# A two-layer diffusion backbone: the last two expert groups combined in one accumulation, and the next layer's sum of squares taken behind the branch

## The chip, the cores and the metric
The kernel runs on 1 core of a Trainium2 chip. The metric is the device time of one execution in microseconds (us); lower is better. Before the change the median of 3 runs is 1619.9 us (1619.38 to 1620.89).

## The reference
Two layers act on 256 latent tokens and 256 context tokens of width 1024. Each layer norms and modulates its input, projects it, runs three token mixers, adds the result to the stream, norms again and runs a mixture of 32 experts. Cut to what the change touches:

```python
for l in range(DEPTH):                       # 2
    h = modulate(rms_norm(x, g_norm[l, 0]), sh1, sc1)
    y = token_mixers(h, hc, w_in[l], ...)    # h @ w_in first
    x = x + gt1 * y
    h = modulate(rms_norm(x, g_norm[l, 1]), sh2, sc2)
    x = x + gt2 * hier_moe(h, ...)           # top-1 group, top-2 experts
```

`rms_norm` needs the sum of x*x over the 1024 features of every token; `hier_moe` is the sum over experts of weight times SwiGLU expert. The context tokens go through the same steps in layer 0, with their own modulation.

## The kernel before
The stream x is held transposed in SBUF, as eight slices (k or f = 0 to 7) of 128 features by 512 tokens, in buffers named qkv. `mixers(l, ...)` does the norm, the projections and the mixers; `moe(l, ...)` does the experts. The order of instructions on each engine is set by a scheduler that simulates the program as it is recorded; the order of the code is only its starting point. SP issues the weight loads, in its own order.

**The experts.** Tokens are gathered into fixed slots, four experts to a group q, eight groups. `gate_up`, `swiglu`, `act_T` and `down(q)` (L1375) give each expert's rows `ys[q, v_]`, split in two parts; `combine(q)` (L1266) multiplies them by the scatter matrix `Cs[q]` into PSUM (L1275, TensorE, PE), and VectorE (DVE) adds the scaled result to x (L1280): 16 adds for a group of layer 0. The loop over q (L1403) runs `down(q - 1)` and `combine(q - 1)` inside group q; `down` and `combine` of the last group follow it (L1428, L1429).

**The end of layer 0.** Behind the last combine stand the preparation of layer 1's first weight chunk, win[1, 12] (L1431: split in whi by ScalarE, ACT, L230, and wlo by DVE, L231), and two `mod_chunk` (L1432 to L1435). A `mod_chunk` makes a piece of the modulation vectors: 8 matmuls of the conditioning with a weight tile (L247), a copy by ACT (L250), a pair of transposes (L252) and two small DVE operations (L256, L257). More chunks are put between later projections. In the trace one of these fp32 matmul instructions leaves two records.

**The overflow branch.** If a slot overflows, all experts are computed densely (the `If` of L1440). All engines test the same value and jump over the body when nothing overflows, as here. An engine passes the branch when its own work ahead of it is issued.

**The sum of squares.** `Stats.step` (L276) squares one slice on ACT (L279, L282) and adds it to `acc` (L286) on DVE or, for every second slice, on GpSimd (POOL). For layer 1 `combine` of the last group of layer 0 calls it after each slice of x is final (L1282), so it lies ahead of the branch, and the body of the branch does it again:

```python
                if nxt[0] is not None:
                    nxt[0].step(xT[f])
```

`Stats.cols` sums over the features by matmuls with ones (L295), then DVE (L299) and POOL (L302, the power -1/2); `Stats.rows` spreads the result over the partitions (L310) and ACT copies it to SBUF (L314). This is r, the row of 1/rms.

**The start of layer 1** (L474 to L485). x is written to DRAM as xs by two DMAs on ACT's queue (L1510). `scaled` makes h0 and l0, the two parts of x times the norm's gain and modulation, without r (L379 on ACT, L380 on DVE), so that the projection with win[1, 12] (48 matmuls L343, L344, L345 on qkv with whi and wlo; `mm3` does hi*hi, hi*lo, lo*hi) can run before r is known; its result is multiplied by r when it is read out (L730, then L754). `shift_share` (L409, L413, L415, L417) gives what the shift adds to it. `shifted` makes the normed h proper, in two parts hh and hl: x times r (L332, on DVE and POOL in turn), scale and shift (L337 on ACT, L339 on DVE), the split (L388 on ACT, L389 on DVE). All later projections of the layer read h; the first of them is with chunk win[1, 13]. SP loads three modulation weights into buffers y (L737) and three into wraw (L213) meanwhile.

Of the kernel before, what the change touches and what calls it, by code (L numbers as in the profile page):

```python
# [11 lines left out]
F32R = mybir.dt.float32r  # L12
# [7 lines left out]
DEPTH = 2  # L20
D = 1024
LAT = 256
CTX = 256
N = LAT + CTX
KT = D // 128
# [20 lines left out]
def tile_backbone(ctx: ExitStack, tc: tile.TileContext, T, out):  # L46
# [316 lines left out]
    def prep(src):  # L363
        return wsplit(wraw(src, [KT, 256]), [KT, 256])

    def mixers(l, need_ctx, xsrc, stats):
        nq = N if need_ctx else LAT
        ntq = nq // 128

# [52 lines left out]
        if l == 0:  # L422
            def mod_w(m, tag):
                w = s8(tag, [KT, 256]) if tag else wraw(T["wmod"][0, m], [KT, 256])
                if tag:
                    nc.sync.dma_start(w, T["wmod"][0, m])
                return w

            def split(w, hi, lo):
                for i in range(0, KT, 2):  # L430
                    h, o = (t.tiles[i // t.per][:, i % t.per:i % t.per + 2] for t in (hi, lo))
                    nc.scalar.copy(h, w[:, i:i + 2])
                    nc.vector.tensor_sub(o, w[:, i:i + 2], h.bitcast(F32))
                return hi, lo

            X[0] = x = slabs("mg", N)

            def load_x2(i):
                nc.sync.dma_start(x.tiles[i // 2][:, 2 * (i % 2):2 * (i % 2) + 2], T["xT"][:, 2 * i:2 * i + 2])

            wm = {4: mod_w(4, "h")}
            w0 = wraw(win[12], [KT, 256])
            load_x2(0)
            wm[5] = mod_w(5, "h")
            load_x2(1)
            w1 = wraw(win[13], [KT, 256])
            load_x2(2)
            wm[6] = mod_w(6, "h")
            load_x2(3)
            wm[7] = mod_w(7, "h")  # L450
            h0 = Slabs([s8("qkv", [4, N], F32R) for _ in range(2)], 4)
            l0 = Slabs([s8("qkv", [4, N], F32R) for _ in range(2)], 4)
            stats = Stats(N, False)
            mod_chunk(0, 4, pat, wm[4])
            pre_w = [split(w0, Slabs([s8("qkv", [KT, 256], F32R)], KT), Slabs([
                tp.tile([128, 4, 256], F32R, tag="PT", name=nm("wl"), bufs=PTB) for _ in range(2)], 4))]
            for j in range(4):
                if j > 0:
                    mod_chunk(0, 4 + j, pat, wm[4 + j])
                scaled((2 * j, 2 * j + 1))  # L460
                if j == 1:
                    pre_w.append(split(w1, Slabs([s8("y", [KT, 256], F32R)], KT),
                                       Slabs([s8("y", [KT, 256], F32R)], KT)))
                for k in (2 * j, 2 * j + 1):
                    stats.step(x[k], False)
            r = stats.rows(stats.cols(pao()), "acc", 1)
            hh, hl = full_norm()
            for j in range(4):
                mod_chunk(0, j, pat, mod_w(j, None))
                shift_parts(slice(2 * j, 2 * j + 2))  # L470
                shifted((2 * j, 2 * j + 1))
            for c in range(len(pre_w)):
                shift_share(c, pre_w[c])
        else:  # L474
            x = X[0]
            h0 = Slabs([s8("qkv", [4, N], F32R) for _ in range(2)], 4)
            l0 = Slabs([s8("qkv", [4, N], F32R) for _ in range(2)], 4)
            shift_parts(slice(0, KT))
            w, A = lead.pop()
            pre_w = [w]  # L480
            scaled(range(KT), A)
            r = stats.rows(stats.cols(pao()), "acc", 1)
            shift_share(0, pre_w[0])
            hh, hl = full_norm()
            shifted(range(KT), A)  # L485
# [265 lines left out]
        for f in shares:  # L751
            for v_ in range(2):
                c = slice(256 * v_, 256 * v_ + 256)
# [251 lines left out]
        xT = X[0]  # L1005
# [155 lines left out]
    def moe(l, nt, st, rt):  # L1161
# [99 lines left out]
                    nc.vector.scalar_tensor_tensor(  # L1261
                        htl[i][:, j, c], rt.tok[i][:, j, c], r, hth[i][:, j, c].bitcast(F32), op0=ALU.mult, op1=ALU.subtract)
        ys, Cs, ths = {}, {}, {}
        nxt = [None]

        def combine(q):  # L1266

            if l == 0 and q == NQ - 1:
                nxt[0] = Stats(nt, False)
            for f in range(KT):  # L1270
                p = pmm()
                for v_ in range(ns):
                    c = slice(256 * v_, 256 * v_ + 256)
                    for part in range(2):
                        nc.tensor.matmul(  # L1275
                            p[:, c], lhsT=ys[q, v_][:, part, 128 * f:128 * f + 128], rhs=Cs[q][:, c],
                            start=(part == 0), stop=(part == 1))
                for v_ in range(ns):
                    c = slice(256 * v_, 256 * v_ + 256)
                    nc.vector.scalar_tensor_tensor(  # L1280
                        xT[f][:, c], p[:, c], modT[l][:, 40 + f, v_:v_ + 1], xT[f][:, c], op0=ALU.mult, op1=ALU.add)
                if nxt[0] is not None:  # L1282
                    nxt[0].step(xT[f])
                if l == DEPTH - 1 and q == NQ - 1 and f % 2 == 1:
                    emit(f - 1)

# [88 lines left out]
        def down(q, aT):  # L1375
            wd = fetched.pop(("down", q))
            for v_ in range(ns):
                ys[q, v_] = s8("mg", [2, D], F32R)
            for cc in range(2):
                c = slice(512 * cc, 512 * cc + 512)  # L1380
                for v_ in range(ns):
                    yp = pmm()
                    for kk in range(2):
                        for e in range(4):
                            nc.tensor.matmul(
                                yp[CAP * e:CAP * e + CAP], lhsT=aT[:, v_, kk, CAP * e:CAP * e + CAP],
                                rhs=wd[cc][kk][e], start=(kk == 0), stop=(kk == 1))
                    split_psum(ys[q, v_][:, 0, c], ys[q, v_][:, 1, c], yp)
# [14 lines left out]
        for q in range(NQ):  # L1403
# [11 lines left out]
            fetch_down(l, q + 1)  # L1415
            if q > 0:
                down(q - 1, aT)
                combine(q - 1)
            if q + 1 < NQ:
                scatter_mats(q + 1)  # L1420
            if o < 3:
# [4 lines left out]
                if q % 2 == 1:  # L1426
                    xe = xe_next
        down(NQ - 1, act_T(NQ - 1))  # L1428
        combine(NQ - 1)  # L1429
        if l == 0:  # L1430
            lead.append((prep(T["win"][1, 12]), norm_scale(1, 0, slice(0, KT))))  # L1431
            for _ in range(2):  # L1432
# [7 lines left out]
        with tc.If(top >= 1024 + CAP):  # L1440
# [14 lines left out]
            with tc.For_i(0, NQ, 1) as q4:  # L1455
                for e in range(4):
# [29 lines left out]
                    for f in range(KT):  # L1486
# [5 lines left out]
                        for v_ in range(nt // 256):  # L1492
                            c = slice(256 * v_, 256 * v_ + 256)
                            nc.vector.scalar_tensor_tensor(
                                xT[f][:, c], p[:, c], modT[l][:, 40 + f, v_:v_ + 1], xT[f][:, c], op0=ALU.mult, op1=ALU.add)
            if nxt[0] is not None:
                nxt[0].n = 0
                for f in range(KT):
                    nxt[0].step(xT[f])
            else:  # L1500
                for f in range(0, KT, 2):
                    emit(f)
        return nxt[0]

    st, rt = mixers(0, True, T["xT"], None)
    st = moe(0, N, st, rt)
    sp = ctx.enter_context(tc.tile_pool(name="spill", bufs=1, space=bass.MemoryType.DRAM))
    xs = sp.tile([128, KT, N], F32, name="xs")
    for i in range(2):
        nc.scalar.dma_start(xs[:, 4 * i:4 * i + 4], X[0].tiles[i])  # L1510
    st, rt = mixers(1, False, xs, st)
    moe(1, LAT, st, rt)


# [100 lines left out]
```

## Time and profile before
| what | value |
|---|---|
| median of 3 runs | 1619.9 us (1619.38 to 1620.89) |
| profiled execution | 1621.5 us, span of the trace 1619.6 us |
| mean granted TensorE clock | 0.96 |
| PE busy | 1498.1 us, 92% of the span |
| DVE busy | 778.6 us, 48% |
| ACT busy | 593.8 us, 37% |
| POOL busy | 171.0 us, 11% |
| DMA | 349.26 MB, mean 216 GB/s |

The span runs from the first to the last instruction; the execution's own time holds what lies around it, 1.9 us here. A busy share is an average over stages: what a wait costs is read from the timeline of its own stretch. [...] In the timeline a row is a run of like instructions: start, length, engine, line, operation, output and input tiles, count, and in brackets the idle time ahead of it with what ended it.

### The profile page before, as it was taken

The page shows a single profiled execution, that of the slowest core. Times are in us where ns is not written, and L with a number is a line of the kernel's source. Part 1 is how long each engine was busy: PE and PEld are TensorE (multiplying, and loading weights), DVE is VectorE, ACT ScalarE, POOL GpSimd, SP SyncE. Part 2 cuts the span into 40 slices and gives each one's busy share as a digit, 9 for nine tenths or more (in the row PEclk, how much of TensorE's full clock was granted, in tenths as well). Part 3 has the DMA queues.
Part 4 walks back from the last instruction along what each step waited for, and adds up shares of the span by engine and source line. Part 5 has one row for each costly group of instructions (what it writes and reads, how often), then busy time and mean ns, then how long its engine had stood idle before and what let it go on. Part 6 is the DMA issues. An engine that isn't in the chain of part 4 may idle for free. (4 is left out here: it accounts for less than half of the span.)

```text
span 1619.6 us, 25921 instructions
## 1 busy us (share of the span) xinstructions
PE 1498.1 (92%) x10609; PEld 1050.0 (65%) x10609; DVE 778.6 (48%) x1767; ACT 593.8 (37%) x1197; POOL 171.0 (11%) x154
## 2 busy tenths in 40 slices
PE   5999999999999979979999996999999999797886
PEld 3688889777767758844434444888988889632221
DVE  4626953443355336253333447359455656432222
ACT  4424642433433333332212225346355555311110
POOL 2201220000032003000000003003110222000000
PEclk9999999999999988989999998999999999899887
DMA  8544323333223215159899977642243547699998
GB/s 305 184 161 149 111 84 131 119 129 130 79 92 104 83 48 205 53 188 393 360 380 421 394 336 268 215 173 85 79 143 129 184 155 299 232 418 425 423 426 334
DMA packets 57199, 349.26 MB, mean 216 GB/s; under 512 B 6912, under 2 KB 8032, under 8 KB 20336
## 3 DMA queue, kind: packets, MB, share of 16 engines
q1 hardware_dynamic: 54720, 341.02, 54.9%
q10 hardware_dynamic: 1616, 5.24, 0.9%
q0 software_dynamic: 736, 1.24, 0.5%
q8 instruction: 88, 1.44, 0.4%
q14 instruction: 39, 0.32, 0.1%
HBM read 344.33 MB, written 3.15 MB: 215 GB/s over the span
## 5 line engine op out<-in xcount | busy, mean ns | idle before, releaser
L231 DVE TENSOR_TENSOR wlo<-wraw,whi 128x1024 fp32r<-128x1024 f32 (+1 forms) x152 | 188.3, 1241 | 170.5 <-ACT whi L230 166.3
L343 PE MATMUL mm<-h,whi 128*128 128x512 f32 (+1 forms) x656 | 226.4, 347 | 1.1 <-DVE t L703 0.6
L344 PE MATMUL mm<-h,whi 128*128 128x512 f32 (+1 forms) x656 | 223.3, 342 | 0.0
L345 PE MATMUL mm<-h,wlo 128*128 128x512 f32 (+1 forms) x656 | 221.9, 343 | 0.1
L230 ACT CAST whi<-wraw 128x1024 fp32r<-128x1024 f32 (+1 forms) x152 | 155.6, 1026 | 159.8 <-PE mm L344 71.3
L344 PE MATMUL mm<-wlo,h 128*128 128x256 f32 (+1 forms) x640 | 184.3, 289 | 0.0
L343 PE MATMUL mm<-whi,h 128*128 128x256 f32 (+1 forms) x640 | 182.8, 289 | 0.0
L345 PE MATMUL mm<-whi,h 128*128 128x256 f32 (+1 forms) x640 | 181.9, 286 | 0.0
L343 PEld LDWEIGHTS mm<-h,whi 128*128 128x128 f32 x656 | 123.8, 189 | 29.4 <-issue 11.1
L345 PEld LDWEIGHTS mm<-h,wlo 128*128 128x128 f32 x656 | 123.1, 189 | 23.6 <-issue 9.5
L344 PEld LDWEIGHTS mm<-h,whi 128*128 128x128 f32 x656 | 124.2, 189 | 16.8 <-issue 4.8
L343 PEld LDWEIGHTS mm<-whi,h 128*128 128x128 f32 x640 | 121.4, 191 | 4.6 <-issue 3.7
L344 PEld LDWEIGHTS mm<-wlo,h 128*128 128x128 f32 x640 | 122.2, 191 | 1.8 <-issue 1.7
L345 PEld LDWEIGHTS mm<-whi,h 128*128 128x128 f32 x640 | 121.9, 191 | 1.6 <-issue 1.4
L1350 PE MATMUL at<-qkv,y 128*32 128x512 f32 x792 | 104.8, 615 | 6.5 <-DMA qkv<-in_wgu 6.5
L1280 DVE SCALAR_TENSOR_TENSOR qkv<-mm,c_modT,qkv 128x256 f32<-128x256 f32 x192 | 80.5, 477 | 36.5 <-PE mm L1275 36.5
L636 ACT ACTIVATE a<-at,nmx 128x512 f32<-128x512 f32 (+1 forms) x96 | 59.0, 617 | 93.9 <-DVE nmx L634 93.7
L634 DVE TENSOR_REDUCE nmx<-at 128x1 f32<-128x512 f32 (+1 forms) x96 | 55.9, 597 | 56.1 <-PE at L617 52.7
L1350 PE MATMUL at<-wraw,y 128*32 128x512 f32 x552 | 74.1, 623 | 8.4 <-DMA wraw<-in_wgu 8.4
L1358 DVE SCALAR_TENSOR_TENSOR a<-a,at 128x256 f32<-128x256 f32 x24 | 10.1, 421 | 136.2 <-ACT a L1357 136.2
L1357 ACT ACTIVATE a<-at 128x256 f32<-128x256 f32 x24 | 9.2, 384 | 178.8 <-PE at L1350 178.3
L1316 ACT ACTIVATE y<-mm,c_modT 128x256 f32<-128x256 f32 x96 | 40.3, 472 | 93.2 <-PE mm L1311 90.8
(388 smaller groups left out, 2547.5 us busy)
## 6 DMA issues: line engine op xcount, KB each, us to landing
qkv<-in_wgu SPq DMA_DIRECT2D x62, 1024.0 KB, 11.5
wraw<-in_win SPq DMA_DIRECT2D x56, 1024.0 KB, 4.9
wraw<-in_wgu SPq DMA_DIRECT2D x42, 1024.0 KB, 11.7
wraw<-in_wmod SPq DMA_DIRECT2D x39, 1024.0 KB, 5.0
qkv<-in_wdn SPq DMA_DIRECT2D x31, 1024.0 KB, 9.5
wraw<-in_wdn SPq DMA_DIRECT2D x19, 1024.0 KB, 11.1
h<-in_wgu SPq DMA_DIRECT2D x14, 1024.0 KB, 17.3
wraw<-in_wbr SPq DMA_DIRECT2D x24, 512.0 KB, 3.3
```

Of the source, the lines that this page charges most:

```text
L230: nc.scalar.copy(hv, src)
L231: nc.vector.tensor_sub(lv, src, hv.bitcast(F32))
L343: nc.tensor.matmul(out_, lhsT=lh, rhs=rh, start=first, stop=False)
L344: nc.tensor.matmul(out_, lhsT=lh, rhs=rl, start=False, stop=False)
L345: nc.tensor.matmul(out_, lhsT=ll, rhs=rh, start=False, stop=last)
L634: nc.vector.tensor_reduce(nmx[:, hf:hf + 1], S[qt][hf], axis=AX.X, op=ALU.max, negate=True)
L636: nc.scalar.activation(P[qt][hf], S[qt][hf], AF.Exp, bias=nmx[:, hf:hf + 1], scale=1.0, accum_out=sm[:, hf:hf + 1])
L1280: nc.vector.scalar_tensor_tensor(xT[f][:, c], p[:, c], modT[l][:, 40 + f, v_:v_ + 1], xT[f][:, c], op0=ALU.mult, op1=ALU.add)
L1316: nc.scalar.activation(xe[:, k], p[:, 256 * (k % 2):256 * (k % 2) + 256], AF.Identity, bias=modT[l][:, 24 + k, v_:v_ + 1])
L1350: nc.tensor.matmul(gps[v_][CAP * e:CAP * e + CAP], lhsT=xe[v_][:, k, s0:s0 + CAP], rhs=w[e], start=(k == 0), stop=(k == KT - 1))
L1357: nc.scalar.activation(th[:, 0:256], gp[:, 0:256], AF.Tanh, bias=0.0, scale=0.5)
L1358: nc.vector.scalar_tensor_tensor(th[:, 0:256], th[:, 0:256], 1.0, gp[:, 0:256], op0=ALU.add, op1=ALU.mult)
```

## The change
- `combine` takes several groups. In layer 0 `combine(6)` is no longer called behind `down(6)`; at the end `combine(6, 7)` adds both groups into one PSUM tile, 8 matmuls to a half slice in place of 4 and 4, and DVE reads it out once. The tiles of `ys[7]` go into the slots "qkv" and "y", since those of group 6 are still in use.
- `moe` makes no sum of squares for the next layer, neither in `combine` nor in the body of the branch. `mixers(1, ...)` makes it behind the branch: for each slice `scaled`, then `Stats.step` with its adds on DVE alone.

The lines of the changed kernel are 3 higher from L481 to about L1264 (L733 was L730, L757 was L754, L740 was L737).

```diff
@@ mixers, layer 1
             pre_w = [w]
-            scaled(range(KT), A)
+            stats = Stats(N, False)
+            for k in range(KT):
+                scaled((k,), A[:, k:k + 1])
+                stats.step(x[k], False)
             r = stats.rows(stats.cols(pao()), "acc", 1)
@@ combine
-        nxt = [None]
-        def combine(q):
-            if l == 0 and q == NQ - 1:
-                nxt[0] = Stats(nt, False)
+        def combine(*qs):
+            q = qs[-1]
             for f in range(KT):
                 p = pmm()
                 for v_ in range(ns):
                     c = slice(256 * v_, 256 * v_ + 256)
-                    for part in range(2):
+                    for i, (qq, part) in enumerate((qq, part) for qq in qs for part in range(2)):
                         nc.tensor.matmul(
-                            p[:, c], lhsT=ys[q, v_][:, part, 128 * f:128 * f + 128], rhs=Cs[q][:, c],
-                            start=(part == 0), stop=(part == 1))
+                            p[:, c], lhsT=ys[qq, v_][:, part, 128 * f:128 * f + 128], rhs=Cs[qq][:, c],
+                            start=(i == 0), stop=(i == 2 * len(qs) - 1))
...
-                if nxt[0] is not None:
-                    nxt[0].step(xT[f])
@@ down
-                ys[q, v_] = s8("mg", [2, D], F32R)
+                ys[q, v_] = s8(("qkv", "y")[v_] if l == 0 and q == NQ - 1 else "mg", [2, D], F32R)
@@ the loop over groups, and behind it
                 down(q - 1, aT)
-                combine(q - 1)
+                if l == DEPTH - 1 or q < NQ - 1:
+                    combine(q - 1)
...
-        combine(NQ - 1)
+        combine(*((NQ - 2, NQ - 1) if l == 0 else (NQ - 1,)))
@@ the body of the branch
-            if nxt[0] is not None:
-                nxt[0].n = 0
-                for f in range(KT):
-                    nxt[0].step(xT[f])
-            else:
+            if l == DEPTH - 1:
                 for f in range(0, KT, 2):
                     emit(f)
```

The order on PE behind the branch, before: `acc` is the sum of squares, `at` of L409 the shift share, `s1p` the reciprocal root.

```order
L1440 UNCONDITIONAL_BRANCH x2
L295 MATMUL ao_9085<-c_ones,acc_8249 128x1 x4
L409 MATMUL at_9101<-whi_8330,spad_9044 32x256
L409 MATMUL at_9101<-wlo_8331,spad_9044 32x256
...
L409 MATMUL at_9101<-wlo_8335,spad_9044 32x256
L343 MATMUL mm_9204<-qkv_9046,whi_8330 128x512
L343 MATMUL mm_9205<-qkv_9046,whi_8330 128x512
L310 MATMUL ao_9094<-c_ident,s1p_9091 128x128 x4
L344 MATMUL mm_9204<-qkv_9048,whi_8330 128x512
```

The same place after the change, to the end of the first projection:

```order
L409 MATMUL at_9055<-wlo_8288,spad_8975 32x256
L343 MATMUL mm_9158<-qkv_8977,whi_8283 128x512
L343 MATMUL mm_9159<-qkv_8977,whi_8283 128x512
L344 MATMUL mm_9158<-qkv_8979,whi_8283 128x512
L345 MATMUL mm_9158<-qkv_8977,wlo_8284 128x512
L344 MATMUL mm_9159<-qkv_8979,whi_8283 128x512
L345 MATMUL mm_9159<-qkv_8977,wlo_8284 128x512
L247 MATMUL at_9227<-y_9152,c_cpad 32x256 x8
L343 MATMUL mm_9158<-qkv_8977,whi_8283 128x512
...
L345 MATMUL mm_9159<-qkv_8978,wlo_8288 128x512
L295 MATMUL ao_9039<-c_ones,acc_8984 128x1 x4
```

L295 went from ahead of the 16 matmuls of L409 to behind the 48 matmuls of the projection, and one modulation chunk, on the first loaded buffer y, stands behind the first six of them.

PE between the first projection and the stream of win[1, 13] (whi_9354 before), before the change:

```order
L247 MATMUL at_9303<-y_9202,c_cpad 32x256 x8
L247 MATMUL mm_9337<-wraw_9335,c_cpad 32x256 x8
L252 MATMUL at_9303<-c_ident,t_1654_9312 128x128 x2
L252 MATMUL mm_9320<-c_ident,t_1657_9329 128x128 x2
L252 MATMUL mm_9337<-c_ident,t_1660_9346 128x128 x2
L343 MATMUL mm_9362<-h_9123,whi_9354 128x512
L344 MATMUL mm_9362<-h_9125,whi_9354 128x512
L343 MATMUL mm_9363<-h_9123,whi_9354 128x512
L344 MATMUL mm_9363<-h_9125,whi_9354 128x512
L345 MATMUL mm_9362<-h_9123,wlo_9355 128x512
```

The same place after the change (whi_9308 is win[1, 13]):

```order
L295 MATMUL ao_9039<-c_ones,acc_8984 128x1 x4
L247 MATMUL at_9242<-y_9154,c_cpad 32x256 x8
L310 MATMUL ao_9048<-c_ident,s1p_9045 128x128 x4
L247 MATMUL mm_9212<-wraw_9210,c_cpad 32x256 x8
L247 MATMUL mm_9274<-wraw_9272,c_cpad 32x256 x8
L247 MATMUL mm_9291<-wraw_9289,c_cpad 32x256 x8
L343 MATMUL mm_9316<-h_9077,whi_9308 128x512
L344 MATMUL mm_9316<-h_9079,whi_9308 128x512
L345 MATMUL mm_9316<-h_9077,wlo_9309 128x512
```

The six pairs L252 and the set L247 of the third buffer y are gone from ahead of the stream; they now stand among its matmuls. Only two of its matmuls stand ahead of its first L345, where four did.

DVE from r to the first split of win[1, 13], after the change (a2 is x times r, h_1603 and h_1604 are the halves of hl; of each kind one or two rows):

```order
L332 TENSOR_TENSOR a2_1610_9096<-qkv_990_5590,acc_1598_9053 128x512
L733 SCALAR_TENSOR_TENSOR qkv_1624_9150<-mm_1629_9158,acc_1598_9053 128x512
L733 SCALAR_TENSOR_TENSOR qkv_1624_9150<-mm_1630_9159,acc_1598_9053 128x512
...
L757 TENSOR_SCALAR qkv_1624_9150<-qkv_1624_9150,shb_1581_8976 128x256 x2
...
L389 TENSOR_TENSOR h_1603_9079<-t2_1611_9102,h_1601_9077 128x512
...
L339 TENSOR_SCALAR t2_1619_9130<-a2_1620_9131,smp_1430_8291,c_modT1_135 128x256
L231 TENSOR_TENSOR wlo_1648_9309<-wraw_1646_9306,whi_1647_9308 128x1024
```

Before, the first L231 of this chunk stood behind all eight L389, both L730, the four L754 and the small operations of the modulation chunks; it now stands behind four L389, both L733 and the four L757, and the other four L389 follow it.

## Rows read from the trace of the kernel before
**Rows 1.** The page, costliest groups: busy us, mean ns | idle before, its releaser.
```profile
L343 PE MATMUL mm<-h,whi 128*128 128x512 f32 (+1 forms) x656 | 226.4, 347 | 1.1 <-DVE t L703 0.6
```
**Rows 2.** Timeline of PE, 967 to 1013: start us, length us, work, [idle before].
```profile
967.47 3.82 PE L1275 MATMUL mm<-wlo,mg 128*128 128x256 f32 x24
981.41 1.87 PE L295 MATMUL ao<-c_ones,acc 128*128 128x1 f32 x8 [10.12 <-DVEq L1440]
983.20 1.10 PE L409 MATMUL at<-whi,spad 128*32 128x256 f32 x8
...
986.53 0.73 PE L343 MATMUL mm<-qkv,whi 128*128 128x512 f32 x2
...
998.84 1.93 PE L247 MATMUL at<-y,c_cpad 128*32 128x256 f32 x32
...
1010.03 0.45 PE L252 MATMUL at<-c_ident,t 128*128 128x128 f32 x2
1010.32 0.74 PE L252 MATMUL mm<-c_ident,t 128*128 128x128 f32 x4
1011.57 0.50 PE L343 MATMUL mm<-h,whi 128*128 128x512 f32 x1 [0.51 <-ACT whi L230]
...
1012.83 0.74 PE L345 MATMUL mm<-h,wlo 128*128 128x512 f32 x2
```
**Rows 3.** Instructions of L1440: ns min/median/max, first and last start us.
```profile
L1440 PEldq COMPARE_BRANCH  x1: 3601/3601/3601, 971.2 to 971.2; - x1
...
L1440 DVEq EVENT_SEMAPHORE  x1: 21/21/21, 981.3 to 981.3; - x1
```
**Rows 4.** Timeline of DVE, 979 to 1012.
```profile
979.30 1.49 DVE L286 TENSOR_TENSOR acc<-acc,a 128x512 f32<-128x512 f32 x2 [1.44 <-POOL acc L286]
...
990.05 1.28 DVE L332 TENSOR_TENSOR a<-qkv,acc 128x512 f32<-128x512 f32 x2
...
997.80 0.40 DVE L339 TENSOR_SCALAR t<-a,smp,c_modT 128x256 f32<-128x256 f32 x1
...
1003.39 0.68 DVE L730 SCALAR_TENSOR_TENSOR qkv<-mm,acc 128x512 f32<-128x512 f32 x1
1004.00 0.68 DVE L389 TENSOR_TENSOR h<-t,h 128x512 fp32r<-128x512 f32 x1
...
1005.20 1.13 DVE L754 TENSOR_SCALAR qkv<-qkv,shb 128x256 f32<-128x256 f32 x4
...
1011.55 2.36 DVE L231 TENSOR_TENSOR wlo<-wraw,whi 128x1024 fp32r<-128x1024 f32 x2
```
**Rows 5.** Timeline of SP, the loads of y.
```profile
977.92 1.28 SPq L737 DMA_DIRECT2D y<-in_wmod  x3
```
**Rows 6.** These three loads, from issue to landing.
```profile
DMA to landing us min/median/max: 4.9/8.1/13.2
```
**Rows 7.** Timeline of ACT, the copy that makes r.
```profile
989.14 0.57 ACT L314 COPY acc<-ao 128x512 f32<-128x512 f32 x1
```
**Rows 8.** Groups by shape, 971.3 to 1011.6: busy us, mean ns | idle before.
```profile
L379 ACT ACTIVATE qkv<-qkv,smp 128x256 fp32r<-128x256 f32 x16 | 6.5, 495 | 4.7 <-DMA y<-in_wmod 4.7
...
L339 DVE TENSOR_SCALAR t<-a,smp,c_modT 128x256 f32<-128x256 f32 x8 | 5.8, 769 | 0.0
L389 DVE TENSOR_TENSOR h<-t,h 128x512 fp32r<-128x512 f32 x8 | 5.2, 679 | 0.0
...
L282 ACT ACTIVATE a<-qkv 128x512 f32<-128x512 f32 x4 | 2.5, 630 | 4.0 <-DVE acc L286 1.8 <-DVE qkv L1280 1.4 <-POOL acc L286 0.8
...
L302 POOL TENSOR_TENSOR s1p<-s1p,c_powm 128x4 f32<-128x4 f32 x1 | 1.0, 1033 | 4.3 <-DVE s1p L299 4.3
```
**Rows 9.** Windows: stretch, its length, busy us of PE, PEld, DVE, ACT, POOL, clock, DMA share, GB/s.
```profile
972.50:976.00 3.50, 0.00 (x0) 0.00 (x0) 3.50 (x7) 1.46 (x3) 0.14 (x1) 1.00 0.02 5
...
982.80:986.20 3.40, 3.40 (x32) 1.86 (x34) 2.65 (x8) 3.40 (x10) 1.03 (x1) 0.50 0.94 294
986.20:989.60 3.40, 3.40 (x25) 2.70 (x18) 3.40 (x9) 3.40 (x9) 0.00 (x0) 1.00 0.99 410
```

More of the change, by code (lines that the diff above doesn't have):

```diff
@@ L364, in prep, with mixers @@
         return wsplit(wraw(src, [KT, 256]), [KT, 256])
-    def mixers(l, need_ctx, xsrc, stats):
+    def mixers(l, need_ctx, xsrc):
         nq = N if need_ctx else LAT
@@ L1495, in moe @@
                                 xT[f][:, c], p[:, c], modT[l][:, 40 + f, v_:v_ + 1], xT[f][:, c], op0=ALU.mult, op1=ALU.add)
-            if nxt[0] is not None:
-                nxt[0].n = 0
-                for f in range(KT):
-                    nxt[0].step(xT[f])
-            else:
+            if l == DEPTH - 1:
                 for f in range(0, KT, 2):
                     emit(f)
-        return nxt[0]
-    st, rt = mixers(0, True, T["xT"], None)
-    st = moe(0, N, st, rt)
+    st, rt = mixers(0, True, T["xT"])
+    moe(0, N, st, rt)
     sp = ctx.enter_context(tc.tile_pool(name="spill", bufs=1, space=bass.MemoryType.DRAM))
@@ L1510, in tile_backbone @@
         nc.scalar.dma_start(xs[:, 4 * i:4 * i + 4], X[0].tiles[i])
-    st, rt = mixers(1, False, xs, st)
+    st, rt = mixers(1, False, xs)
     moe(1, LAT, st, rt)
```

## The prediction
> **What bounds the kernel now.** I read the page first. TensorE (PE) does the long projections of both layers with hardly any wait: 656 matmuls of one line waited 1.1 us in all [rows 1]. A change outside those projections is therefore worth the time by which it moves their start, and work that is pushed in among them costs its whole length. So the question is a narrow one: the change touches the end of layer 0 and the first 40 us of layer 1, from 971 to 1013 us of the span, and what counts is when the stream of layer 1's second weight chunk (called win13 here: L343 to L345 on h with whi and wlo) gets going, and what runs inside it.
>
> The timeline of PE over that stretch shows this [rows 2]. PE ends the last combine at 971.29 (967.47 + 3.82). Then it stands for 10.12 us until VectorE (DVE) has passed the branch. It resumes at 981.41 with the column sums of the squares (L295), 983.20 the shift share (L409), 986.53 the 48 matmuls of the first projection on h0, and from 998.84 the modulation chunks (L247, L252). win13 starts at 1011.57, its first L345 at 1012.83. Of the 10.12 us, PE's own branch takes 3.60 us (3601 ns) [rows 3]; DVE comes through the branch only at 981.3, since the last adds of the sum of squares end at 980.79 after a wait of 1.44 us for POOL [rows 4]. All of L247 and L252 between 998.84 and 1011 lies in a hole that PE would have had anyway, because DVE makes h until 1004.7.
>
> **The change part by part.** My times are against the profiled execution, 1621.5 us with a span of 1619.6; the median of the three runs shown is 1619.9, 1.6 lower.
>
> *The joint combine.* 32 + 32 matmul instructions of combine(6) and combine(7) become 64 in one accumulation: PE's work stays. Sixteen DVE adds (L1280) go. They lie beside PE work and ahead of a wait, so I give them no price of their own; they count in when DVE reaches the branch. PE's end moves a little: two modulation chunks that stood among the matmuls now come last, and the last pair of transposes waits for ScalarE's (ACT) copy, about 0.7 us by my estimate from a pair's 0.29 [rows 2] and a copy as long again. So PE ends at 972.0.
>
> *The sum of squares.* Eight squares and the adds leave the stretch ahead of the branch. DVE and ACT get through it some 7 us sooner, and PE's wait becomes its own branch: 972.0 + 3.6 = 975.6, against 981.4. Behind the branch ACT makes sixteen scaled pieces (6.5 us) and eight squares at 0.63 [rows 8], 11.5 us from about 974, so the sum is there by about 986, earlier than anyone reads it.
>
> *Who reads it, and when.* PE's order behind the branch decides. Before, L295 was first, and r (the row of 1/rms, ACT L314) was ready at 989.14 + 0.57 = 989.71 [rows 7]. Now L295 stands behind all 48 matmuls of the first projection, and ahead of 42 of them there is a modulation chunk (L247) on the tile y, which must come by DMA. Step by step:
> - 975.6, then the shift share 986.53 - 983.20 = 3.33 at the half clock it had [rows 2]: 978.9. Six matmuls at 0.24: 980.3.
> - y: its issue waited for ACT and PE to pass the branch and came at 977.92 [rows 5]; now PE's 975.6 is last. The three loads took 4.9, 8.1 and 13.2 us [rows 6]. The copies of x to the spill buffer are now issued ahead of them and share the engines, so I put the first near the middle load, 7.5 us: 983.2. PE waits 2.9 us.
> - L247 0.96 (half of the 1.93 for two sets), 42 matmuls at 0.24 (998.84 - 986.53 for 48 and the small ones between, shortened for those): 994.2.
> - L295 983.20 - 981.41 = 1.79: 996.0. Then DVE's L299 and POOL's L302 at 1.03 [rows 8], 1.4 together: 997.4. L310 0.8, the copy 0.6, with handing over: r at 998.9, **9.2 us later** than before.
>
> From r on DVE sets the pace. Before, from its first L332 at 990.05 to 1003.39 [rows 4] it took 13.34 us for four L332, eight L339, seven L389. Now ahead of the first split of win13 (L231) stand three L389 fewer (3 x 0.68) [rows 8], but two L733 (0.68 each, then L730) and four L757 (1.13, then L754) and that L231 (half of 2.36): 13.34 - 2.0 + 1.4 + 1.1 + 1.2 = 15.0 us. With 0.3 from r to the first L332: first L345 at 998.9 + 0.3 + 15.0 = 1014.2, against 1012.83. **Term a: +1.4.** The 9.2 us are nearly all covered, because before the h slices were done at 1004.7 and waited there.
>
> That cover is what is used up. **Term c: +0.5**: four matmuls of win13 ran ahead of its first L345 before, two do now. **Term b: +2.7**: one L247 set (0.96) and six pairs of L252, at 0.29 each (1010.32 - 1010.03) [rows 2], stood in the hole; now they stand among win13's matmuls. **Term d: +2.4**: the hole itself is now empty. PE has its last L247 done near 1002 and waits until about 1013. [...] win13 began at full clock before, since L247 and L252 ran just ahead. 4.8 us at half speed lose 2.4.
>
> Sum: 1.4 + 0.5 + 2.7 + 2.4 = **+7.0 us**, 1628.5 for a profiled execution, **1626.9** for the median. Later projections start by that much later, and I see no wait behind them that takes it up [rows 1].
>
> Bounds. a: -1.2 if y lands as fast as the fastest load (4.9), -4.2 if DVE also meets nothing of POOL (worked out under (ii)), up to +2.9 if y lands 1.5 later. b: 1.8 if half of the pairs fall into waits of win13, 3.2 if a pair costs half of 0.74. c: 0 to 1. d: 0 if the hole is not long enough, 3.4 at most (a clock that stays down 6.8 us, two slices of [rows 9]). Together -2.4 to +10.5.
>
> [...] PE's branch took 3.60 us in the row [rows 3], and in the sum it now lies open, since nobody holds PE longer. [...] The body that is jumped over is the same on PE, so I stay with the row.
>
> **The rivals.**
> (i) *No change.* y lands in about 4.9 us and the clock holds or comes back at once: a = -1.2, b + c = 2.5, d = 0, so +1.3, 1621. For it: 4.85 us is the row's fastest. Against it: that load was issued before any other traffic.
> (ii) *Faster.* PE's earlier restart (5.8 us) is kept as far as win13. It takes y in 4.9 (r 2.6 sooner, 996.3) and a DVE stretch free of POOL: its eight L339 averaged 0.77 us [rows 8], the undisturbed one took 0.40 [rows 4], 8 x 0.37 = 3.0. Then the first L345 comes at 1008.6, a = -4.2; with b at its low end and c and d at nothing, -2.4, and -4 if the L332 on DVE gain as well (about 1616). It decides if the first L345 comes ahead of 1008. Against it: POOL keeps the four L332 that disturb DVE.
> [...]
> (iv) *The change doesn't do what it says*: the scheduled order could put PE's end or the branch elsewhere, for instance if POOL or ACT come to the branch late. The order shows nothing left for them to do there; little chance.
>
> **How the numbers follow.** The forecast has 0.55, (iii) 0.17, (i) 0.15, (ii) 0.10, (iv) 0.03. What a measurement here can tell from no change is 0.2%, 3.2 us. The forecast's lower end and half of (iv) reach into that. Faster 0.10, within 0.2% 0.18, slower 0.72. The range is 1617.5 to 1632.0: it takes in (i), the forecast with the bounds of its terms and most of (iii), and leaves out (ii) and the far end of the sum.
>
> **What would show it.** Right: PE's first row behind the branch is L409 near 975.6; a wait of about 3 us for the DMA of y near 980; L295 near 994, r near 999; an empty PE between about 1002 and 1013; granted clock 0.50 in the first 4 or 5 us of win13; L252 rows among its matmuls. Wrong: PE restarting at 981 (the sum of squares was not what held it); L295 ahead of 990; first L345 ahead of 1010 (then a is negative and (ii) is near); clock 1.00 at win13's start; or a gap further on that takes the delay up.

## The result, and the profile after

The change makes the kernel slower: 1629.89 us (median of 7 runs, 1626.86 to 1632.18) against 1619.86 us (7 runs); ratio 1.0065, 95% interval 1.0048 to 1.0082, that is +7.8 to +13.3 us. The forecast was 1626.9. The profiled execution took 1630.11 us with a span of 1628.2, against 1621.5 and 1619.6.

The page of the changed kernel says nothing of this loss: PE's and DVE's busy times are a little lower than before, and so is ACT's.

```profile
span 1628.2 us, 25890 instructions
...
PE 1496.8 (92%) x10609; PEld 1047.4 (64%) x10609; DVE 773.6 (48%) x1754; ACT 593.0 (36%) x1197; POOL 168.0 (10%) x151
```

PE's timeline shows it. These rows answer to [rows 2]:

```profile
971.68 0.44 PE L252 MATMUL at<-c_ident,t 128*128 128x128 f32 x2 [0.49 <-ACT t L250]
976.08 1.10 PE L409 MATMUL at<-whi,spad 128*32 128x256 f32 x8 [3.96 <-PEq L1440]
...
981.52 0.58 PE L409 MATMUL at<-wlo,spad 128*32 128x256 f32 x1 [1.80 <-issue]
...
983.36 1.22 PE L343 MATMUL mm<-qkv,whi 128*128 128x512 f32 x2
...
986.22 1.08 PE L247 MATMUL at<-y,c_cpad 128*32 128x256 f32 x8
...
997.83 0.94 PE L295 MATMUL ao<-c_ones,acc 128*128 128x1 f32 x8
...
1004.99 1.07 PE L247 MATMUL mm<-wraw,c_cpad 128*32 128x256 f32 x16 [1.81 <-DVE qkv L733]
1015.21 0.79 PE L343 MATMUL mm<-h,whi 128*128 128x512 f32 x1 [9.15 <-ACT whi L230]
...
1016.47 0.79 PE L345 MATMUL mm<-h,wlo 128*128 128x512 f32 x1
...
1018.35 0.45 PE L343 MATMUL mm<-h,whi 128*128 128x512 f32 x1
...
1026.99 1.07 PE L247 MATMUL at<-y,c_cpad 128*32 128x256 f32 x16
...
1031.69 0.36 PE L343 MATMUL mm<-h,whi 128*128 128x256 f32 x1
```

PE resumes at 976.08, the wait of 10.12 us is down to 3.96, and yet win13's first L345 comes at 1016.47 in place of 1012.83. Between lie L295 at 997.83 (981.41 before) and a hole of 9.15 us ahead of win13. A chunk's L247 at 1026.99 now stands among win13's matmuls.

The branch, in the rows that answer to [rows 3]: PE's own jump again takes 3.5 us, and it is now the last; DVE is through before it.

```profile
L1440 ACTq COMPARE_BRANCH  x1: 45/45/45, 971.8 to 971.8; - x1
...
L1440 PEldq COMPARE_BRANCH  x1: 3492/3492/3492, 972.3 to 972.3; - x1
...
L1440 DVEq EVENT_SEMAPHORE  x1: 21/21/21, 975.1 to 975.1; - x1
```

DVE's timeline from r to the split of win13, beside [rows 4]:

```profile
1001.97 2.37 DVE L332 TENSOR_TENSOR a<-qkv,acc 128x512 f32<-128x512 f32 x2 [2.99 <-ACT acc L314]
...
1011.05 2.48 DVE L389 TENSOR_TENSOR h<-t,h 128x512 fp32r<-128x512 f32 x4
1013.45 1.37 DVE L339 TENSOR_SCALAR t<-a,smp,c_modT 128x256 f32<-128x256 f32 x4
1015.20 2.36 DVE L231 TENSOR_TENSOR wlo<-wraw,whi 128x1024 fp32r<-128x1024 f32 x2 [0.37 <-ACT whi L230]
```

and ACT's, beside [rows 7]: the splitting of win13 (L230) stands behind four L337, and the first of these waits for DVE.

```profile
1001.35 0.59 ACT L314 COPY acc<-ao 128x512 f32<-128x512 f32 x1 [13.34 <-PE ao L310]
...
1011.76 2.47 ACT L337 ACTIVATE t<-a,c_modT,smp 128x256 f32<-128x256 f32 x4 [2.69 <-DVE h L389]
1014.14 1.98 ACT L230 CAST whi<-wraw 128x1024 fp32r<-128x1024 f32 x2
```

The granted clock (the share of full speed that the profile gives for TensorE, the third column from the right, as in [rows 9]; at 1.00 the 128x512 matmuls of this trace step by 0.23 us, at 0.50 by 0.43): from the restart it stays at 0.50 for 11.6 us, until within the slice that begins at 986.20 (a mean of 0.78 there puts the rise at about 987.7), and it is at 0.50 again when win13 starts.

```profile
972.50:976.00 3.50, 0.00 (x0) 0.00 (x0) 0.41 (x3) 0.00 (x0) 0.00 (x0) 0.72 0.08 26
...
982.80:986.20 3.40, 3.40 (x8) 1.83 (x6) 3.40 (x8) 3.40 (x10) 0.00 (x0) 0.50 0.99 417
986.20:989.60 3.40, 3.40 (x24) 2.00 (x24) 2.90 (x6) 1.81 (x4) 0.00 (x0) 0.78 1.02 427
...
1013.50:1017.00 3.50, 1.75 (x3) 1.00 (x4) 3.13 (x7) 3.44 (x6) 0.00 (x0) 0.50 0.00 0
```

A profile's absolute times scatter: over the traces of this case the last gate_up of layer 0 ends anywhere between 933.5 and 942.5 us. So all kernels are compared from that matmul on, in four parts: to PE's first matmul behind the branch; to the end of ACT's L314 (r); to win13's first L345; to the first 128x256 matmul of the next projection. For the kernel before that is 942.5 (935.48 + 7.05, the last L1350), 981.41, 989.71, 1012.83, 1024.07.

| kernel (us) | to the restart | to r | to win13's L345 | to the 128x256 | sum | measured against before, 95% |
|---|---|---|---|---|---|---|
| before | 38.9 | 8.3 | 23.1 | 11.2 | 81.5 | 1 |
| the change | 34.6 | 25.9 | 14.5 | 15.2 | 90.2 | 1.0065 (1.0048 to 1.0082) |
| e1: sum moved, groups apart | 33.6 | 21.3 | 13.1 | 17.0 | 85.0 | 1.0024 (1.0007 to 1.0041) |
| e2: joint combine alone | 33.7 | 8.6 | 21.6 | 11.2 | 75.1 | 0.9989 (0.9968 to 1.0010) |
| e3: change, L295 earlier | 33.4 | 27.2 | 12.8 | 15.9 | 89.3 | 1.0059 (1.0038 to 1.0080) |
| e4: e2, adds on DVE alone | 34.0 | 9.5 | 22.4 | 11.2 | 77.2 | 0.9966 (0.9949 to 0.9983) |
| e5: change, spill late | 34.3 | 24.3 | 14.1 | 16.3 | 89.0 | 1.0079 (1.0056 to 1.0103) |
| e6: change, code shifted | 33.8 | 27.8 | 14.5 | 16.0 | 92.1 | one run, 1631.67 us |
| e7: change, r early | 34.6 | 18.8 | 17.0 | 16.2 | 86.7 | 1.0052 (1.0032 to 1.0072) |
| e8: change, hole filled | 33.2 | 24.5 | 14.6 | 15.8 | 88.1 | one run, 1625.4 us |
| e9: e7 and e5 | 33.5 | 21.4 | 17.1 | 15.0 | 87.0 | 1.0050 (1.0029 to 1.0072) |
| e10: before, adds on DVE alone | 38.7 | 8.3 | 23.0 | 11.2 | 81.2 | 0.9999 (0.9984 to 1.0015) |
| e11: e4, spill late | 34.1 | 7.6 | 22.8 | 11.2 | 75.8 | 0.9956 (0.9937 to 0.9975) |
| e12: e11, chunks behind win13 | 33.2 | 7.5 | 17.5 | 19.0 | 77.2 | 0.9996 (0.9980 to 1.0012) |

The change's +8.7 in these parts agrees with the spans' +8.6. What follows the 128x256 matmul, to the end of the span, took 595.4 to 598.0 us in every trace but that of e12, where it took 600.8; why is not shown. One of e12's 12 runs took 2006.1 us at a mean granted clock of 0.69, against 0.96 to 0.97 in the others, and its ratio leaves it out.

### The profile page after: what moved, and what is told of

Its sections match the earlier page's. It is cut to its first block, busy times and chain, and to the rows that moved or that the text cites. A ratio compares the mean times of both kernels' runs of the same rounds, so it can differ in the third digit from the quotient of the medians.

```text
span 1628.2 us, 25890 instructions
## 1 busy us (share of the span) xinstructions
PE 1496.8 (92%) x10609; PEld 1047.4 (64%) x10609; DVE 773.6 (48%) x1754; ACT 593.0 (36%) x1197; POOL 168.0 (10%) x151
## 3 DMA queue, kind: packets, MB, share of 16 engines
q0 software_dynamic: 736, 1.24, 0.4%
## 5 line engine op out<-in xcount | busy, mean ns | idle before, releaser
L231 DVE TENSOR_TENSOR wlo<-wraw,whi 128x1024 fp32r<-128x1024 f32 (+1 forms) x152 | 188.3, 1241 | 168.4 <-ACT whi L230 163.7
L345 PE MATMUL mm<-h,wlo 128*128 128x512 f32 (+1 forms) x656 | 222.5, 344 | 0.0
L230 ACT CAST whi<-wraw 128x1024 fp32r<-128x1024 f32 (+1 forms) x152 | 155.5, 1026 | 163.2 <-PE mm L344 73.2
L345 PE MATMUL mm<-whi,h 128*128 128x256 f32 (+1 forms) x640 | 181.9, 286 | 0.0
L343 PEld LDWEIGHTS mm<-h,whi 128*128 128x128 f32 x656 | 124.2, 190 | 37.8 <-ACT whi L230 11.2
L345 PEld LDWEIGHTS mm<-h,wlo 128*128 128x128 f32 x656 | 123.5, 190 | 23.9 <-issue 9.5
L345 PEld LDWEIGHTS mm<-whi,h 128*128 128x128 f32 x640 | 121.9, 191 | 1.6 <-issue 1.4
L1281 DVE SCALAR_TENSOR_TENSOR qkv<-mm,c_modT,qkv 128x256 f32<-128x256 f32 x176 | 73.8, 477 | 37.0 <-PE mm L1276 36.9
## 6 DMA issues: line engine op xcount, KB each, us to landing
qkv<-in_wgu SPq DMA_DIRECT2D x62, 1024.0 KB, 11.2
wraw<-in_wgu SPq DMA_DIRECT2D x42, 1024.0 KB, 11.6
```

What stands on the lines that cost most here:

```text
L230: nc.scalar.copy(hv, src)
L231: nc.vector.tensor_sub(lv, src, hv.bitcast(F32))
L343: nc.tensor.matmul(out_, lhsT=lh, rhs=rh, start=first, stop=False)
L345: nc.tensor.matmul(out_, lhsT=ll, rhs=rh, start=False, stop=last)
L1281: nc.vector.scalar_tensor_tensor(xT[f][:, c], p[:, c], modT[l][:, 40 + f, v_:v_ + 1], xT[f][:, c], op0=ALU.mult, op1=ALU.add)
```

## The experiments

My theory was that the moved sum of squares costs the time: it is read late, the cover ahead of win13 is used up, and chunk work and half clock come into win13. The rivals were the joint combine itself, and traffic or code loading behind the branch.

**One part of the change at a time.** e1 is the kernel before with the sum moved:

```diff
-            scaled(range(KT), A)
+            stats = Stats(N, False)
+            for k in range(KT):
+                scaled((k,), A[:, k:k + 1])
+                stats.step(x[k], False)
```

> Only the sum of squares is moved behind the branch; the last two groups are combined apart, as before. If the loss comes from where the sum of squares is read (r late, chunk work pushed in among win13's matmuls, half clock at win13's start), nearly all of it stays: +7 to +11 us over the kernel before, first L345 of win13 some 3 us later. If the joint combine and its slots cost the time: within 3 us of the kernel before.

Measured +1.1 to +6.6 us: the direction was right, the size was not. Nor did win13's first L345 come 3 us later: it stands 68.0 us behind the last gate_up, 70.3 in the kernel before. So e1 loses nothing up to win13. Its loss lies from that L345 to the 128x256 matmul, 17.0 us in place of 11.2: the chunk work stands among win13's matmuls, and the granted clock is 0.50 for the first ones.

```profile
1002.27 0.80 PE L343 MATMUL mm<-h,whi 128*128 128x512 f32 x1 [4.01 <-ACT whi L230]
```
```profile
1006.80:1010.20 3.40, 2.95 (x7) 2.37 (x8) 3.40 (x7) 2.73 (x5) 0.00 (x0) 0.50 0.24 31
```

The table shows the same for every kernel with the sum moved: 15.0 to 17.0 us in this part, and 11.2 in every one with the sum ahead of the branch but e12.

e2 has `combine(NQ - 2, NQ - 1)` with the sum left in `combine`:

```diff
-        combine(NQ - 1)
+        combine(*((NQ - 2, NQ - 1) if l == 0 else (NQ - 1,)))
```

> Only the joint combine; the sum of squares stays ahead of the branch, on ACT, DVE and POOL as before. If the loss comes from the moved sum: no loss, rather a gain of 1 to 5 us over the kernel before, since sixteen adds fewer let DVE reach the branch near 976 in place of 981 and L295 still comes first behind it. If the joint combine costs the time: +5 to +10 us.

No loss beyond +1.6 us, and no gain that can be told from none (-5.2 to +1.6); in its trace the restart comes 5.2 us sooner, as expected. DVE tests the branch early, and PE's own jump of 3.5 us ends last:

```profile
L1442 PEldq COMPARE_BRANCH  x1: 3496/3496/3496, 963.5 to 963.5; - x1
...
L1442 DVEq COMPARE_BRANCH  x1: 72/72/72, 966.0 to 966.0; - x1
```

So the joint combine shows no cost, and as a rival for the whole loss it is out. But the parts do not add: e1 and e2 give +3.5 and -6.4 in the stretch, both together +8.7. The table says where. The early restart is there once only: moving the sum alone brings 33.6, joining alone 33.7, both 34.6. And the part from the restart to r is 21.3 in e1 but 25.9 with both. In e1 the sixteen adds still hold DVE, so ACT, which issues the copies of x when DVE is through, comes after SP's loads of y, which go out when PE's jump ends (0.1 us behind it in both traces). SP's row and ACT's row of e1:

```profile
971.40 2.38 SPq L740 DMA_DIRECT2D y<-in_wmod  x3
```
```profile
972.70 0.82 ACTq L1503 DMA_DIRECT2D xs<-qkv  x2
```

With both, the copies (975.12) go ahead of y (975.95):

```profile
975.95 2.33 SPq L740 DMA_DIRECT2D y<-in_wmod  x3
```
```profile
975.12 1.77 ACTq L1505 DMA_DIRECT2D xs<-qkv  x2
```
```profile
DMA to landing us min/median/max: 9.0/13.5/14.7
```

The first y took 9.0 us to land, against 6.3 in e1 and 4.9 in [rows 6].

**Who held DVE before.** e4 is e2 with `step(xT[f], False)`, e10 the kernel before with the same word: no add of the sum on POOL.

> As the run with the joint combine only, but all adds of the sum of squares on DVE, none on POOL. If POOL's adds (1.27 us each, and DVE waits for them) still hold DVE ahead of the branch, 1 to 3 us faster than with POOL; if PE's own branch of 3.6 us is by then the last to arrive, the same within 1 us.

> The kernel before with one word changed: all adds of the sum of squares on DVE, none on POOL, the groups combined apart. If POOL's two adds on the path hold DVE ahead of the branch, DVE reaches it 2 to 3 us sooner and the kernel gains 1 to 3 us. If the sixteen adds of L1280 that the joint combine saves are what counts, it gains less than 1 us.

e4 is 0.9966 of before and cannot be told from e2 (the intervals overlap). e10 gains nothing; DVE still ends the wait at 978.93:

```profile
978.93 1.87 PE L295 MATMUL ao<-c_ones,acc 128*128 128x1 f32 x8 [9.60 <-DVEq L1440]
```

So it was DVE's sixteen adds, not POOL's two on the path, that held the branch (to the restart 33.7 us in e2, 38.7 in e10): what the joint combine saves is real in e4, with the sum ahead of the branch and its adds on DVE.

**Traffic and code behind the branch.** e5 moves the two copies of x:

```diff
+            with tc.issue_after(stats.sq.ins):
+                for i in range(2):
+                    nc.scalar.dma_start(xsrc[:, 4 * i:4 * i + 4], x.tiles[i])
             r = stats.rows(stats.cols(pao()), "acc", 1)
...
-    for i in range(2):
-        nc.scalar.dma_start(xs[:, 4 * i:4 * i + 4], X[0].tiles[i])
```

> The changed kernel with the two copies of x to the spill buffer issued behind ACT's last square, not right behind the branch. If the 2 MB that they write ahead of y's loads and of PE's code make PE stand (1.8 us in the middle of L409) and hold its clock down, the stall goes, y lands some 5 us after its issue, the projection ends 4 to 7 us sooner behind the branch and the kernel gains 3 to 6 us on the change: +4 to +7 over the kernel before. If they cost nothing, the same as the change within 2 us.

e6 adds, in the body that is jumped over, 32 matmuls into a tile that nothing reads:

```diff
+            for _ in range(32):
+                q = ptr()
+                nc.tensor.matmul(q[:, :128], lhsT=ident, rhs=ident, start=True, stop=True)
```

> The changed kernel with 32 more matmuls in the body of the branch that is jumped over, so that nothing more is executed but PE's code behind the branch lies elsewhere. If the stall in L409 comes from where the code behind the jump lies, it is gone or at another instruction, and L409's first to the projection's end takes 3 to 6 us less than the 21.7 of the change. If it comes from the traffic alone, it stays at 1.5 to 3 us in L409.

The stall is gone in both. In e6 that gains nothing: from L409's first to L295 it takes 23.7 us, where 3 to 6 less than 21.7 was expected. PE then comes to y early and waits for it, which the change's trace had hidden behind the stall:

```profile
976.28 1.13 PE L409 MATMUL at<-wlo,spad 128*32 128x256 f32 x8
...
984.30 1.93 PE L247 MATMUL at<-y,c_cpad 128*32 128x256 f32 x16 [4.59 <-DMA y<-in_wmod]
```

In e5 the first y lands after 5.2 us, PE does not wait for it, and L295 comes 17.6 us behind the restart in place of 21.7, as expected. But the kernel is not faster (1.0079 against 1.0065, intervals overlapping; +9.1 to +16.7 us, where +4 to +7 was expected). The scheduler, which orders the program anew for every edit, has put a chunk's L247 that waits for its weights ahead of L310:

```profile
991.64 0.95 PE L295 MATMUL ao<-c_ones,acc 128*128 128x1 f32 x8
...
995.54 1.07 PE L247 MATMUL mm<-wraw,c_cpad 128*32 128x256 f32 x16 [1.09 <-DMA wraw<-in_wmod]
996.54 1.16 PE L310 MATMUL ao<-c_ident,s1p 128*128 128x128 f32 x8
```

4.9 us from L295 to L310, 2.3 in the change. My expectation missed since it took the rest of the order as given.

What ends the stall is not in PE's rows, but the DMA queues of the trace give a sign of it. One of them, q8, is of the kind that the profile calls `instruction`. In the change no packet of it begins between 976.0 and 979.2; one begins at 979.22 and ends at 980.17, and PE goes on at 981.52. Its row for 979.2 to 980.2:

```profile
q8 instruction: 1, 0.02, 5.9%
```

| trace | copies of x ahead of the restart, us | restart to that packet, us | packet's end to PE's resuming, us | stall, us |
|---|---|---|---|---|
| the change | 0.96 | 3.14 | 1.35 | 1.80 |
| e3 | 1.24 | 4.32 | 1.24 | 2.86 |
| e8 | 1.22 | 3.17 | 1.29 | 1.76 |
| e7 | 0.79 | 1.65 | 1.43 | 0.64 |
| e2 | 0.54 | 0.60 | - | 0 |
| e6 | 0.49 | 0.43 | - | 0 |
| e5 | behind it | 0.45 | - | 0 |
| e9 | behind it | 0.94 | - | 0 |

In the other six traces the packet begins at most 0.3 us behind the restart, and there is no stall. So PE stands where this packet is late, and resumes a nearly constant time behind it (1.24 to 1.43 us); and the packet is late where the copies went out 0.79 us or more ahead of the restart. That q8 brings PE's code is my reading of the queue's kind and of these times; no row shows it. In e6 the copies went out only 0.49 us ahead, so e6 does not show whether the code's place or that moment took the stall away.

**r early.** e3 put L295 behind 24 of the 48 matmuls (`issue_after` of the second half on the last L295); e7 put L310 there too, the last adds of the sum ahead of L417, and the chunks on y behind L310:

```diff
+                    with tc.issue_after(behind.ins) if behind is not None and k >= 4 else nullcontext():
-                    mm3(pp[i][:, :nt], ...)
+                        mm3(pp[i][:, :nt], ...)
```

> The changed kernel with PE's order altered behind the branch: the column sums L295 stand behind 24 of the 48 matmuls of the first projection, and the modulation chunks on y behind L310. If L295's place and the wait for y make r late, r comes near 993 to 995 in place of 1001.9 and the kernel loses 3 to 8 us less than the change: +2 to +7 over the kernel before. If only the work among win13's matmuls and the clock there count: within 3 us of the change, about +8 to +11.

> The changed kernel with L295 and L310 both ahead of the second 24 matmuls of the projection, the last adds of the sum ahead of L417 on DVE, and the chunks on y behind L310. If r's lateness is what makes win13 late, r comes 5 to 8 us sooner behind the branch than in the change, the first L345 of win13 4 to 7 us sooner, and the kernel loses 4 to 7 us less: +3 to +6 over the kernel before. If win13's start hangs on something else (win13's own load, ACT's order), no gain over the change.

e3 tests nothing: L310 stood behind the other 24, and r came 27.2 us behind the restart. e7 does what it should. In its rows L295 waits for the last add and L310 for POOL; r comes 7.1 us and win13's L345 4.5 us sooner than in the change (70.5 against 75.0 from the last gate_up).

```profile
982.40 1.72 PE L295 MATMUL ao<-c_ones,acc 128*128 128x1 f32 x8 [1.88 <-DVE acc L286]
985.49 2.07 PE L310 MATMUL ao<-c_ident,s1p 128*128 128x128 f32 x8 [1.38 <-POOL s1p L302]
...
1005.23 0.80 PE L345 MATMUL mm<-h,wlo 128*128 128x512 f32 x1 [0.59 <-DVE wlo L231]
```

It stays at +5.2 to +11.6 us: the trace's gain of 3.5 us is within what the runs leave open. e9 joins e7 and e5:

> Both orders together: the changed kernel with L295 ahead of the second half of the projection and the copies of x to the spill buffer behind ACT's last square. If r's lateness, the stall and y's wait make up the part between the branch and r, it takes some 15 us in place of 25.9, and the kernel comes to within 5 us of the kernel before; it stays above it by the chunk work and the half clock within win13 (16 us from its first L345 to the first 128x256 matmul, against 11.2). If the loss lies elsewhere, it stays at +8 or more.

r came 21.4 us behind the restart and not 15, for a chunk's L247 ahead of L310 waited 4.57 us for its weights. Measured +4.7 to +11.7 us: to within 5 us of the kernel before, as expected, is not shown. In both traces r's lateness is a part of the loss (win13's L345 comes 4.5 and 3.0 us sooner than in the change), and the part behind win13's start (16.2 and 15.0 us against 11.2) stays; in time neither can be told from the change.

**The empty hole.** e8 puts 36 matmuls that nothing reads between L310 and win13.

```diff
+                    pd = pao()
+                    for _ in range(36):
+                        with tc.issue_after(stats.row.ins):
+                            nc.tensor.matmul(pd, lhsT=pre_w[0][0][0][:, 0:128], rhs=h0[0][:, :512], start=True, stop=True)
```

> The changed kernel with 36 more 512-column matmuls, whose result nothing reads, between L310 and win13, where PE stands for some 9 us. If the empty hole is what costs the clock at win13's start (term d), the granted clock is 1.00 there and the stretch from the first L345 of win13 to the first 128x256 matmul shrinks by 1 to 1.5 us from 15.2. If the clock falls anyway or does not matter, it stays at 15.2 within 0.3.

Neither: L345 to the 128x256 matmul is 15.8, no shorter than 15.2 but not within 0.3 of it. The clock is still 1.00 when win13 starts, and falls behind it: PE ends the added work at 1006.78 and stands 2.14 us; from win13's fourth matmul on they step by 0.42 us, not 0.23.

```profile
1005.12 1.66 PE L752 MATMUL ao<-qkv,whi 128*128 128x512 f32 x6
1008.92 0.50 PE L343 MATMUL mm<-h,whi 128*128 128x512 f32 x1 [2.14 <-ACT whi L230]
...
1010.52 0.62 PE L343 MATMUL mm<-h,whi 128*128 128x512 f32 x1
1010.94 0.63 PE L344 MATMUL mm<-h,whi 128*128 128x512 f32 x1
```

So this run does not show the price of term d: work that ended 2.14 us ahead of win13 did not keep the clock. In the kernel before it fell ahead of win13 too, but there the chunk work bore it: these two sets ran at 0.50, and win13 began at 1.00 behind them. A set takes 1.07 us at 1.00.

```profile
1006.54 1.85 PE L247 MATMUL at<-y,c_cpad 128*32 128x256 f32 x16 [0.97 <-DVE c_modT L256]
1008.15 1.95 PE L247 MATMUL mm<-wraw,c_cpad 128*32 128x256 f32 x16
```

**A better version.** e11 is e4 with the copies of x behind the scaled pieces.

> The joint combine with the sum ahead of the branch on DVE, and the copies of x to the spill buffer behind the scaled pieces. If y's landing or the load of PE's code still costs time there, 1 to 3 us faster than with the copies right behind the branch (0.9966 of the kernel before). If r is what counts and is early already, the same within 1.5 us.

0.9956 of before (0.9937 to 0.9975), 4.0 to 10.2 us less than the kernel before by its runs; against e4 the intervals overlap, so the late copies are not shown to help. e12 takes the chunks out of win13's way in the code (the `mod_chunk` of the held tiles and `mod_fill(2)` behind `proj_f(win[13])`).

> As the run before it (joint combine, sum ahead of the branch on DVE, copies of x late), with the modulation chunks on y and the next two issued behind win13's projection in the code. The hole between the first projection and win13 is then bounded by DVE's h alone, and win13's load goes out sooner. If the chain of the chunks holds win13 (ACT's and DVE's small operations in front of its split), r to win13's first L345 takes 14 to 17 us in place of 22.8, the chunk work stands behind win13 (+3 to 4 us), and 2 to 5 us come off on balance: 0.992 to 0.995 of the kernel before. If h itself holds it, no gain within 1.5 us.

The first half came out: 17.5 us from r to win13's L345, 22.8 in e11. The second did not: 0.9996 of the kernel before, where 0.992 to 0.995 was expected. The chunk work stands behind win13 as a block of 7.2 us, and there is no hole to take it; the part from L345 to the 128x256 matmul grows by 7.8 us, more than the 5.3 that were won. That is 1.4 us of the stretch against e11, and another 3.7 lie behind it, unexplained.

```profile
1007.21 2.80 PE L247 MATMUL mm<-wraw,c_cpad 128*32 128x256 f32 x48
...
1014.39 0.39 PE L343 MATMUL mm<-h,whi 128*128 128x256 f32 x1 [0.87 <-ACT whi L230]
```

That is the same lesson as term b, from the other side: the chunk work was free only in the hole that was there anyway.

## Why the prediction was right, and where its steps were off

The direction holds, and the time lies within the range; the median is 3 us above the forecast. The reasons hold in kind. That the terms add up to nearly what was forecast (+7.6 by the trace's own times, +7.0) is in part luck: term a was 2.2 larger, and b, c and d together 1.6 smaller. By its steps:

- *PE's end and the restart* were 972.0 and 975.6; measured 972.12 and 976.08. PE's jump took 3.49 us, 3.60 in [rows 3], and 3.36 to 3.78 in e1 to e4 and e10: the row was right to go by.
- *The stretch to the second part of the projection* was mis-sized in its items. Forecast: L409 3.3 us, then 2.9 us of waiting for y. Measured: L409 7.3 us with a stall of 1.80 that the profile shows no other engine to end, the six matmuls at half speed (983.36 to 986.22), and no wait for y, which had landed at 984.95 by then. L247 on y began at 986.22, forecast 983.2. e6 shows the wait of y (4.59) when the stall is gone. The clock stayed at 0.50 from the restart to about 987.7, where the forecast had the six matmuls and the L247 at full speed; it did not fall a second time there, and the 42 matmuls ran at 1.00.
- *r* came at 1001.94 (forecast 998.9), that is +17.6 in the part from the restart to r, against a forecast of +15.0.
- *From r to the first L345* 14.5 us, forecast 15.3. The DVE count was good; ACT's order, which puts L230 behind four L337, held the last 0.4 us.
- *Term a* thus was +3.6 (1016.47 against 1012.83; +4.7 if both are counted from the last gate_up, 75.0 against 70.3), forecast +1.4: this is the term that was mis-sized, by the stall and the clock ahead of y. *Terms b, c and d* together were +4.0, forecast 5.6. In the rows two matmuls that now stand behind the first L345 are 0.5, which is c; the L247 set takes 1.0, three pairs inside add 0.14 each and three at the end 0.6, so b is 2.0; four matmuls at 0.47 in place of 0.23 (1016.47 to 1018.35) make d 1.0. That leaves 0.5 in no one row. d was smaller than 2.4 as the clock returned 3.1 us after win13's first matmul, not the 4.8 that it took behind the wait of 10.12 us before [rows 2, rows 9], from the restart at 981.41 to 986.2. The prediction did not see that in the kernel before the clock had fallen as well, and had come back in the hole (0.50 from 1007 to 1010, 1.00 from 1011 on).
- *Nothing behind takes it up*: right. The spans differ by 8.6.
- Rival (i) puts b + c at 2.5; by the prediction's own terms they are 3.2, or 2.3 with b at its low end.
- Rival (ii) named the early restart as what could win. e4 and e11 show that this gain is real, but belongs to the joint combine with the sum left where it was. My working gave the joint combine no price of its own: right for the sum of both, but it hid that one half of the change was good.

The stall in L409 was 1.80, 2.86, 1.76 and 0.64 us in the change, e3, e8 and e7, always in the sixteen L409; it was gone with the copies late (e5, e9) and in e6. PE's jump of 3.49 us in the change, too, ends 1.4 us behind the end of a packet of the `instruction` queue q8 (973.29 to 974.41), as the stall ends 1.35 us behind the next one. What holds q8's packet back is not shown; that the copies do is my estimate from the table above. The prediction asked what the copies do to y and left out what they may do to this queue.

What stays open: why that packet came in time in e6, and how much of the +7.8 to +13.3 us goes to each part in time, and not in one profile: e7 and e8, which shorten the parts by 2 to 4 us, are within the scatter of the change.

## What to carry to other kernels

Measure each half of a change by itself: here one half gained (with the sum on DVE, e4) and the other lost, and since both released the same wait, the gain came once. A piece of work that is moved behind a branch is not priced by its own length but by where its reader lands in the new order, and by what else the release of the branch sends off at that moment (here the copies of x and the loads of y). Here the small work that filled a hole was free only as long as the hole was there and it stood ahead of the work that the hole waits for.

## What the runs showed of the hardware

- The clock also fell behind a wait, and not only in one: in e8 it was 1.00 at win13's first matmul, behind 2.14 us without work, and from 1010.5 on the next ones ran at 0.50.
- From PE's restart behind the branch to the clock's rise it took 11.6, 12.8 and 8.7 us in the change, e3 and e8, with stalls of 1.80, 2.86 and 1.76 us in between, and 2.8 to 7.6 us in the ten traces without a stall (4.8 in the kernel before [rows 9]). In e7 it took 3.0, and the stall of 0.64 came behind the rise. That the stalls prolonged it is not shown apart from that.
- PE stood up to 2.86 us in a run of like matmuls right behind a jump, with no engine named as the cause. It went on 1.2 to 1.4 us behind the end of a packet of the `instruction` queue q8 (0.02 MB in its row), which in those traces began 1.65 to 4.32 us behind the restart. Where the packet began within 0.94 us of it, there was no stall.
